# Second block's mixer: keys in three full blocks of 128, attention keys made with features as rows, index gemms first, and a buffer of its own for w_uk

## The chip, the cores and the metric

The kernel runs on one core of one Trainium2 chip. The metric is the device time of one execution in microseconds (us), as the median of several runs. The core's engines run side by side, each through its own queue in order: TensorE (PE, with its weight loads shown as PEld), VectorE (DVE), ScalarE (ACT), GpSimd (POOL), and SyncE (SP), which only issues DMAs. An instruction that waits holds up everything behind it in its own queue.

## What is computed

Two transformer blocks in float32 on 256 tokens of width 1024. The first block has four layers, the second has one, and 16 meta tokens are put ahead of its sequence, so it works on 272 positions. The change touches the second block's mixer, which stands between its two feed-forward stages. Cut to what matters:

```
u = rmsnorm(h, mix_norm) @ w_in                    # [272, 2632]
qa, ka, va, qb, ckv, iq, ik, iw = split(u)         # 512,512,512,512,256,512,64,8 wide

# attention A: 4 heads, two score maps each (m = 0, 1), 64 features per map
qa = rmsnorm(qa.reshape(272, 4, 2, 64), a_q_norm)
ka = rmsnorm(ka.reshape(272, 4, 2, 64), a_k_norm)  # 272 x 8 reciprocal roots
s  = einsum('qhmd,khmd->hmqk', qa, ka) * 64**-0.5 + bias_a   (causal)
p  = softmax(s);  a = p[:, 0] - lam * p[:, 1]
o_a = rmsnorm(a @ va, a_subln) * (1 - lam_init)

# attention B: an index picks 64 keys for each query, then 4 heads on a latent
q_lat = rmsnorm(qb @ w_uk, b_q_norm);  c = rmsnorm(ckv, b_kv_norm)
score = sum_h iw_h * relu(iq_h . ik * 64**-0.5)    (8 heads, causal)
sel   = top_k(score, 64)
p = softmax(q_lat . c[sel] * 256**-0.5 + bias_b);  o_b = (p @ c[sel]) @ w_uv

h = h + concat(o_a, o_b) @ w_out
```

Rows of queries are needed for the 256 tokens only; keys and values for all 272 positions.

## The kernel before, in words

Every large product is done in three passes (`mm3`, lines 225 to 227): the float32 operands are split into a rounded part and a remainder of type fp32r, and hi·hi, hi·lo and lo·hi are added up in PSUM (`acc`, four banks). Weights arrive through SP's queue as `raw` (three buffers of 128x2048); ACT rounds each into `hi` (line 73) and DVE forms `lo` (line 76), four buffers of each, in the order of a fixed plan. Between them stand small float32 matmuls and transposes with PSUM tiles `tp` (four banks).

In the second block the activations are held with the features as rows (`hT2`, `xT`). `FeatNorm.add` (lines 1114 to 1127) makes the next stage's operands for one block of 128 features and adds up the squares for the norm, on POOL (lines 1124 and 1126). `FeatNorm.rstd` turns the sums into the reciprocal root with a power of -0.5 on POOL (line 1142), as a column for each token and, after transposes, as a row `rrow`.

The mixer (`mixer2`) has a list of gemms in the order of `MIXER`: ka, qa, va, ik, iq, ckv, qb. Two forms exist. `gemm_as` puts tokens in rows: a block of 128 tokens is the stationary operand and 512 columns of weights stream past; ka and qa are made so. For ka that is three blocks of tokens (16, 128 and 128 of them, the first also computed as a full block), each with 24 matmuls of 512 columns. `gemm_ws` puts features in rows: 128 columns of weights are stationary, 272 or 256 tokens stream past; all others are made so. After a token-row gemm, `qk_sink` (lines 1571 to 1593) scales by the token's root, squares on ACT, sums by head on DVE (line 1583), takes the power of -0.5 of a 128x8 tile on POOL (line 1588 waits for it; the power itself is line 243 in a helper), multiplies on DVE (line 1588), and flips the block to features as rows with four PE transposes (line 1512).

Next to the gemms run small tasks held by `Tasks`, two steps after every gemm step: the index scores (`select_task`: dots on PE at line 1546, relu on ACT, weighted sum on DVE at 1549, then eight rounds of top-8 and replace for each of two query tiles at lines 1556 and 1557), units of attention A (`unit_a`: scores at line 1699, softmax with DVE line 1651 and ACT line 1652, flips at 1662, product with the values at 1673) and units of attention B (`unit_b`, scores at line 1731). Keys are handled in three parts of 16, 128 and 128 (`key_tiles`). The matrix w_uv is loaded at line 1430 into the buffer `wuk`; w_uk is loaded into the same buffer at line 1806, when the last use of w_uv is over. `finish` flips an output half for the last product with w_out (`mixer_out`).

The order of instructions on each engine is set by a scheduler when the program is built; what the queue order is can be listed from the program, and stands below where it matters.

Of the kernel before, what the change touches and what calls it, by code (L numbers as in the profile page):

```python
# [31 lines left out]

MIXER = ("ka", "qa", "va", "ik", "iq", "ckv", "qb")

# [119 lines left out]
def build(ctx, tc, A, out):  # L154
# [950 lines left out]
    class FeatNorm:  # L1105
# [9 lines left out]
        def add(self, f):  # L1115
            n, src = self.n, self.hT[:, f, self.c0:]
            g = self.g[:, f:f + 1]
            hi, lo = [xT[x][:, f, self.c0:] for x in ("hi", "lo")]
            nc.scalar.activation(hi, src, AF.Copy, scale=g)
            nc.vector.scalar_tensor_tensor(lo, src, g, hi.bitcast(F32), op0=ALU.mult, op1=ALU.subtract)  # L1120
            sq = self.pool.tile([P, KC], F32, tag="sqf", bufs=3, name=nm("sqf"))
            nc.scalar.activation(sq[:, :n], src, AF.Square)
            if f == 1:
                nc.gpsimd.tensor_add(self.sum[:, :n], self.prev[0][:, :n], sq[:, :n])
            elif 1 < f < KT - 1:
                nc.gpsimd.tensor_add(self.sum[:, :n], self.sum[:, :n], sq[:, :n])
            self.prev.append(sq)
# [57 lines left out]
    def bias_rows():  # L1185
# [3 lines left out]
        ra = npool.tile([8, NB_POS + 1], F32, name="ra")  # L1189
        frs = hpool2.tile([8, NB_POS], F32, name="frs")  # L1190
        nc.gpsimd.dma_start(rb, A["rel_bias_2"])
# [178 lines left out]
class Tasks:  # L1370
# [45 lines left out]
def mixer2(tc, nc, A, pool, E):  # L1416
# [21 lines left out]
    def lambda_task():  # L1438
        nc.vector.tensor_scalar(gs, gs, 1.0 - 0.2, None, op0=ALU.mult)
        es = []  # L1440
        for i in range(2):
            lj = pool.tile([P, 512], F32, tag="sq8", bufs=1, name=nm("lj"))[:, :64]
# [124 lines left out]
    def rq():  # L1567
        return pool.tile([P, 512], F32, tag="rq", bufs=5, name=nm("rq"))

    def qk_sink(name, g, dstT, cols):  # L1570
# [22 lines left out]
        return sink  # L1593

    va, vc = {}, {}

    def va_task():
        yield from need("vaT")
        for i, (T, (a, rows)) in enumerate(zip((2, 0, 1), tiles(KC))):
            tp = tp_bank()  # L1600
            for b in range(4):
                nc.tensor.transpose(tp[:rows, P * b:P * b + P], late["vaT"][:, b, a:a + rows], ident)
            va[T] = pool.tile([P, 512], F32, name=f"va{T}")
            nc.scalar.activation(va[T][:rows], tp[:rows], AF.Copy)
            yield True
        tk.flags.add("va")

    def vc_task(T):
        yield from need("cT")
        rows, c0 = ROWS[T], COL[T]  # L1610
        p_ = tp_bank()
        for k in range(2):
            nc.tensor.matmul(p_[:rows], lhsT=cT[:, k, c0:c0 + rows], rhs=wuv[:, k, :], start=k == 0, stop=k == 1)
        vc[T] = pool.tile([P, 512], F32, name=f"vc{T}")
        nc.scalar.activation(vc[T][:rows], p_[:rows], AF.Copy)
        tk.flags.add(("vc", T))
        yield True
# [205 lines left out]
    def gemms():  # L1823
# [47 lines left out]
def _layout(i):  # L1871
# [47 lines left out]
    for n, m in (("va", va), ("qb", qb), ("iq", iq), ("ckv", ckv)):  # L1919
        a["w2_" + n] = stat(m, 256)  # L1920
# [58 lines left out]
```

## Time and profile before

| | us |
|---|---|
| median of 3 runs | 2134.31 (2133.76 to 2134.83) |
| the profiled execution, its own time | 2134.71 |
| its span, first to last instruction | 2132.8 |
| granted TensorE clock over the span, share of full speed | 0.993 |
| the mixer: from the first matmul of ka to the last flip of the norm behind it | 1772.0 to 1943.0 of the span |

PE is busy in 99% of the span, DVE in 71%, ACT in 57% and POOL in 4%. A busy PE is not PE at its peak: matmuls overlap in their pipeline, so what one costs is the distance from its start to the next one's start and not its duration. POOL has 130 instructions in the whole program. Idle time of an engine that nobody waits for costs nothing. In the lists of instructions each row has the start in us from the span's start, the duration (of several rows merged: from the first start to the last end), the engine, the line, the operation, what is written and read with its shape, and in brackets the idle time ahead of it with what ended it.

### The profile page before, as it was taken

The numbers are of one execution on the slowest core, as the hardware profiler recorded it, in microseconds if no ns is written. First come the engines' busy times: TensorE is split into PE (matmuls) and PEld (weight loads), VectorE is DVE, ScalarE is ACT, GpSimd is POOL, SyncE is SP. The second block draws the span as 40 slices with busy tenths as digits, with TensorE's granted clock in tenths as the row PEclk, the third lists the DMA queues.
The fourth block names the chain that finished last, engine by engine and source line by source line (L and its number), as shares of the span: only waits on it lengthen the run. The fifth ranks groups of instructions, "written<-read, shape, count | busy, mean of one in ns | idle before, by whom it ended". The sixth has DMA issues, their size and how long they took to land.

```text
span 2132.8 us, 39626 instructions
## 1 busy us (share of the span) xinstructions
PE 2104.3 (99%) x15582; PEld 1974.8 (93%) x15582; DVE 1507.8 (71%) x3646; ACT 1216.2 (57%) x2355; POOL 95.5 (4%) x130
## 2 busy tenths in 40 slices
PE   8999999999999999999999999999999999999999
PEld 8999989989899889799889999899889998879999
DVE  6665679847799579699666655699666655667663
ACT  6656676635565466476455655666464445665442
POOL 1000000000000001100000000000010012011000
PEclk9999999999999999999999999999999999999999
DMA  7444545545465543155544444355556454414543
GB/s 258 149 151 150 177 148 196 181 159 189 165 217 198 197 163 101 39 192 205 190 160 167 149 151 162 124 214 179 197 159 246 142 177 171 140 50 139 189 152 115
DMA packets 57434, 352.37 MB, mean 165 GB/s; under 512 B 7232, under 2 KB 7776, under 8 KB 29728
## 3 DMA queue, kind: packets, MB, share of 16 engines
q1 hardware_dynamic: 53136, 338.88, 45.8%
q0 software_dynamic: 3824, 10.78, 1.7%
q8 instruction: 123, 2.02, 0.4%
q14 instruction: 63, 0.52, 0.1%
q10 hardware_dynamic: 288, 0.18, 0.0%
HBM read 348.74 MB, written 3.22 MB: 165 GB/s over the span
## 4 chain that ended last, share of the span: by engine, by line
PE 56%; DVE 5%; ACT 1%; POOL 1%; issue 1%; ACTq 0%; POOLq 0%; DVEq 0%
PE acc L225 17%; PE acc L227 17%; PE acc L226 17%; DVE lo L76 1%; DVE cvh L1024 1%; DVE o L1024 1%; POOL s L243 1%; PE tp L1673 1%; PE tp L840 1%; PE tp L782 0%; PE tp L1001 0%; PE tp L827 0%; PE tp L802 0%; PE tp L306 0%; ACT hi L73 0%
## 5 line engine op out<-in xcount | busy, mean ns | idle before, releaser
L76 DVE TENSOR_TENSOR lo<-raw,hi 128x512 fp32r<-128x512 f32 (+2 forms) x1440 | 855.3, 633 | 326.6 <-ACT hi L73 322.7
L73 ACT ACTIVATE hi<-raw 128x1024 fp32r<-128x1024 f32 (+3 forms) x720 | 672.5, 965 | 431.3 <-issue 193.3
L227 PE MATMUL acc<-xhi,lo 128*128 128x256 f32 (+1 forms) x2432 | 690.4, 284 | 0.0
L226 PE MATMUL acc<-xlo,hi 128*128 128x256 f32 (+1 forms) x2432 | 690.1, 284 | 0.0
L225 PE MATMUL acc<-xhi,hi 128*128 128x256 f32 (+1 forms) x2432 | 689.8, 284 | 0.2 <-DVE u L515 0.2
L227 PEld LDWEIGHTS acc<-xhi,lo 128*128 128x128 f32 x2432 | 461.9, 190 | 1.1 <-issue 0.9
L225 PEld LDWEIGHTS acc<-xhi,hi 128*128 128x128 f32 x2432 | 461.4, 190 | 1.0 <-issue 0.4
L226 PEld LDWEIGHTS acc<-xlo,hi 128*128 128x128 f32 x2432 | 459.0, 189 | 1.0 <-issue 0.6
L225 PE MATMUL acc<-hi,xhi 128*128 128x384 f32 (+2 forms) x920 | 317.7, 346 | 1.5 <-ACT xhi L348 1.4
L227 PE MATMUL acc<-hi,xlo 128*128 128x384 f32 (+2 forms) x920 | 307.9, 335 | 0.0
L226 PE MATMUL acc<-lo,xhi 128*128 128x384 f32 (+2 forms) x920 | 306.6, 333 | 0.0
L225 PE MATMUL acc<-hi,hidh 128*128 128x512 f32 x480 | 190.7, 398 | 0.3 <-ACT hidh L230 0.3
L227 PE MATMUL acc<-hi,hidl 128*128 128x512 f32 x480 | 189.6, 395 | 0.0
L226 PE MATMUL acc<-lo,hidh 128*128 128x512 f32 x480 | 189.4, 395 | 0.0
L225 PEld LDWEIGHTS acc<-hi,xhi 128*128 128x128 f32 x920 | 172.8, 188 | 9.8 <-ACT xhi L348 3.2
L227 PEld LDWEIGHTS acc<-hi,xlo 128*128 128x128 f32 x920 | 172.7, 188 | 2.5
L226 PEld LDWEIGHTS acc<-lo,xhi 128*128 128x128 f32 x920 | 173.2, 188 | 1.9
L243 POOL TENSOR_TENSOR s<-s,neghalf 128x1 f32<-128x1 f32 (+5 forms) x56 | 42.4, 759 | 1546.6 <-DVE s L256 1415.2
L225 PEld LDWEIGHTS acc<-hi,hidh 128*128 128x128 f32 x480 | 90.5, 189 | 20.6 <-ACT hidh L230 0.5
L227 PEld LDWEIGHTS acc<-hi,hidl 128*128 128x128 f32 x480 | 90.4, 188 | 19.7
L226 PEld LDWEIGHTS acc<-lo,hidh 128*128 128x128 f32 x480 | 90.5, 188 | 19.3
L225 PE MATMUL acc<-hidh,hi 128*128 128x272 f32 (+1 forms) x352 | 100.6, 286 | 0.0
(342 smaller groups left out, 2534.7 us busy)
## 6 DMA issues: line engine op xcount, KB each, us to landing
raw<-in_ffn_w_in_dram SPq DMA_DIRECT2D x88, 1024.0 KB, 4.9
raw<-in_attn_w_qkv_dram SPq DMA_DIRECT2D x96, 768.0 KB, 4.2
raw<-in_ffn_w_out_dram SPq DMA_DIRECT2D x44, 1024.0 KB, 4.9
raw<-in_ffn_w_gu_dram SPq DMA_DIRECT2D x44, 1024.0 KB, 4.9
raw<-in_ffn_w_dn_dram SPq DMA_DIRECT2D x32, 704.0 KB, 4.1
raw<-in_sc_w_in_dram SPq DMA_DIRECT2D x16, 768.0 KB, 4.2
raw<-in_cc_w_pw_dram SPq DMA_DIRECT2D x12, 1024.0 KB, 4.9
raw<-in_attn_w_o_dram SPq DMA_DIRECT2D x8, 1024.0 KB, 4.9
```

Of the source, the lines that this page charges most:

```text
L73: nc.scalar.activation(hi[:, sl], raw[:, sl], AF.Copy)
L76: nc.vector.tensor_sub(lo[:, s2], raw[:, s2], hi[:, s2].bitcast(F32))
L225: nc.tensor.matmul(o, lhsT=lh[0], rhs=rh[0], start=first, stop=False)
L226: nc.tensor.matmul(o, lhsT=lh[0], rhs=rh[1], start=False, stop=False)
L227: nc.tensor.matmul(o, lhsT=lh[1], rhs=rh[0], start=False, stop=last)
L243: mark["pow"] = nc.gpsimd.tensor_tensor(r[:parts], m[:parts], neghalf[:parts, :w], op=ALU.pow)
L840: nc.tensor.matmul(o[rows, 64 * hh:64 * hh + 64], lhsT=pT[s, T][hh][:, j, rows], rhs=vals if h2 is None else vals[:, c, hh, :], start=i == ...
L1024: nc.vector.scalar_tensor_tensor(d, x, w, other, op0=ALU.mult, op1=ALU.add)
L1673: nc.tensor.matmul(o[:, :P], lhsT=pT[:rows, i, :], rhs=vals[t][:rows, P * hd:P * hd + P], start=i == 0, stop=i == len(kts) - 1)
```

## The change

1. `MIXER` becomes ik, iq, ka, qa, va, ckv, qb: the two gemms of the index come first.
2. ka is made with `gemm_ws`: four groups of 128 features by 272 tokens, each with 24 matmuls. Its norm is done in that form: ACT squares the group (128x272), one float32 matmul with a 0/1 matrix `pair` adds up each head's 64 rows and spreads the sum over them, DVE scales and adds the epsilon (line 1620 of the changed kernel), POOL takes the power of -0.5 of the whole 128x272 tile (line 1621), and DVE multiplies (line 1625). The three flips of ka on PE go. qa stays as it was.
3. Keys are handled in blocks of 128 that begin at 0, 128 and 144 (`KB`). The third overlaps the second in 112 keys, so its first 112 value rows are zeroed on POOL (`value_block`); for the first query tile two blocks do, and the probabilities of keys 144 to 255 are zeroed on POOL.
4. w_uk gets a buffer of its own and is loaded at the start of the mixer, behind w_uv, on POOL's queue.
5. The sums of squares in `FeatNorm.add` move from POOL to DVE (both uses, ahead of the mixer and behind it).
6. To make room, scratch tiles share one buffer with the table `frs` of the bias, and the pool `rq` has four buffers where it had five.

```diff
-MIXER = ("ka", "qa", "va", "ik", "iq", "ckv", "qb")
+MIXER = ("ik", "iq", "ka", "qa", "va", "ckv", "qb")
...
             if f == 1:
-                nc.gpsimd.tensor_add(self.sum[:, :n], self.prev[0][:, :n], sq[:, :n])
+                nc.vector.tensor_add(self.sum[:, :n], self.prev[0][:, :n], sq[:, :n])
             elif 1 < f < KT - 1:
-                nc.gpsimd.tensor_add(self.sum[:, :n], self.sum[:, :n], sq[:, :n])
+                nc.vector.tensor_add(self.sum[:, :n], self.sum[:, :n], sq[:, :n])
...
+    wuk = pool.tile([P, 4, 256], F32, tag="wuk", bufs=1, name="wuk")
+    nc.gpsimd.dma_start(wuk, A["b_w_uk_2"])
...
+    KB = [0, P, KC - P]
+
+    def value_block(name, i, src):
+        t = pool.tile([P, 512], F32, name=f"{name}{i}")
+        nc.scalar.activation(t, src, AF.Copy)
+        if i == 2:
+            for rows in (slice(0, 96), slice(96, 3 * P - KC)):
+                nc.gpsimd.memset(t[rows], 0.0)
+        return t
...
+    def ka_sink(u, ps):
+        nc.vector.tensor_mul(kaT[:, u, :], ps[:, :KC], rrow)
+        tk.add(ka_task(u))
+
+    def ka_task(u):
+
+        k = kaT[:, u, :]
+        sq, R = [pool.tile([P, KC], F32, tag="rl", bufs=3, name=nm("kn")) for _ in range(2)]
+        nc.scalar.activation(sq, k, AF.Square)
+        yield True
+        st = tp_bank()
+        nc.tensor.matmul(st[:, :KC], lhsT=pair, rhs=sq, start=True, stop=True)
+        nc.vector.tensor_scalar(R, st[:, :KC], 1.0 / 64, EPS, op0=ALU.mult, op1=ALU.add)
+        nc.gpsimd.tensor_tensor(R, R, E["neghalf"][:, 0:1].to_broadcast([P, KC]), op=ALU.pow)
+        yield True
+        for _ in range(LAG):
+            yield False
+        nc.vector.scalar_tensor_tensor(k, k, gk, R, op0=ALU.mult, op1=ALU.mult)
+        done_k.append(u)
+        if len(done_k) == 4:
+            tk.flags |= {("ka", t) for t in range(3)}
+        yield True
...
+    def gemm_ka():
+        for u in range(2):
+            yield from gemm_ws("w2_ka", u, 2, 0, lambda t, ps: ka_sink(2 * u + t, ps))
...
         ns = pool.tile([P, KC], F32, tag="ns2", bufs=6, name=nm("ns2"))
+        if n < KC:
+            nc.gpsimd.memset(ns[:, n:2 * P], 0.0)
...
     def gemm_qb():
-        tk.until(("dots", 0), ("dots", 1), ("vc", 0), ("vc", 1), ("vc", 2))
-        wuk = pool.tile([P, 4, 256], F32, tag="wuk", bufs=1, name="wuk")
-        nc.gpsimd.dma_start(wuk, A["b_w_uk_2"])
+        tk.until(("dots", 0), ("dots", 1))
...
-            "ka": lambda: gemm_as("w2_ka", (0, 1, 2), 512, 4, qk_sink("ka", gk, kaT, COL)),
+            "ka": gemm_ka,
```

POOL's queue before, from the powers of the norm ahead of the mixer (`rcol`) on; `s` with 8 columns are the tokens' roots of ka (three) and qa (two):

```order
L1430 DMA wuv<-in_b_w_uv_dram 128x1024
L1142 TENSOR_TENSOR rcol_20516<-s_20524,neghalf 16x1
L1142 TENSOR_TENSOR rcol_20516<-s_20530,neghalf 128x1
L1142 TENSOR_TENSOR rcol_20516<-s_20536,neghalf 128x1
L243 TENSOR_TENSOR s_20642<-s_20640,neghalf 128x8
L243 TENSOR_TENSOR s_20664<-s_20662,neghalf 128x8
L243 TENSOR_TENSOR s_20686<-s_20684,neghalf 16x8
L243 TENSOR_TENSOR s_20768<-s_20766,neghalf 128x8
L243 TENSOR_TENSOR s_20797<-s_20795,neghalf 128x8
L243 TENSOR_TENSOR s_21345<-s_21344,neghalf 16x1
```

The same queue now, behind the load of w_uk and four more memsets of `ns`; `kn` is the tile R of a feature group of ka:

```order
L1695 MEMSET ns_3219_21349 128x112
L1695 MEMSET ns_3223_21357 128x112
L1621 TENSOR_TENSOR kn_20774<-kn_20774,neghalf 128x272
L1621 TENSOR_TENSOR kn_20807<-kn_20807,neghalf 128x272
L1621 TENSOR_TENSOR kn_20850<-kn_20850,neghalf 128x272
L1621 TENSOR_TENSOR kn_20884<-kn_20884,neghalf 128x272
L243 TENSOR_TENSOR s_20980<-s_20978,neghalf 128x8
L243 TENSOR_TENSOR s_21002<-s_21000,neghalf 128x8
L1530 MEMSET va_21265 96x512
L1530 MEMSET va_21265 16x512
L243 TENSOR_TENSOR s_21310<-s_21309,neghalf 16x1
```

Five powers of 8 columns have become two, with four powers of 272 columns ahead of them. DVE's queue now, from the first group of ka to the first index scores; `acc` is the gemm's bank, `lo` the remainder of a weight that a later gemm needs (20889 is va's first weight):

```order
L1609 TENSOR_TENSOR kaT<-acc_20747,rrow_20541 128x272
L1620 TENSOR_SCALAR kn_20774<-tp_20776 128x272
L1625 SCALAR_TENSOR_TENSOR kaT<-kaT,headgains,kn_20774 128x272
L1609 TENSOR_TENSOR kaT<-acc_20780,rrow_20541 128x272
L76 TENSOR_TENSOR lo_20889<-raw_20737,hi_20888 128x512 x2
L1620 TENSOR_SCALAR kn_20807<-tp_20809 128x272
L76 TENSOR_TENSOR lo_20889<-raw_20737,hi_20888 128x512 x2
L1609 TENSOR_TENSOR kaT<-acc_20823,rrow_20541 128x272
L1625 SCALAR_TENSOR_TENSOR kaT<-kaT,headgains,kn_20807 128x272
L1620 TENSOR_SCALAR kn_20850<-tp_20852 128x272
L1625 SCALAR_TENSOR_TENSOR kaT<-kaT,headgains,kn_20850 128x272
L1609 TENSOR_TENSOR kaT<-acc_20856,rrow_20541 128x272
```

Each multiplication at line 1625 waits for POOL's power of its group, and the next group's first step stands behind it: group 2 behind power 1, group 4 behind power 3. Right behind these rows stand the four `lo` of va's second weight, the fourth `kn` (line 1620) and the fourth multiplication (line 1625), and only then the index scores. Before, the same stretch of DVE's queue was, from the first block of ka:

```order
L1583 TENSOR_REDUCE s_20638<-sq_3094_20636 128x8
L247 TENSOR_SCALAR s_20640<-s_20638 128x8
L1588 TENSOR_TENSOR rq_20634<-rq_20634,s_20642 128x512
L1583 TENSOR_REDUCE s_20660<-sq_3099_20658 128x8
L247 TENSOR_SCALAR s_20662<-s_20660 128x8
L1588 TENSOR_TENSOR rq_20656<-rq_20656,s_20664 128x512
```

Here too the multiplication (line 1588) waits for a power, of 8 columns. The buffers of `kn` come from the pool `rl` of three, which the index scores use as well: the third relu of the index takes the buffer of the fourth group's `kn`.

PE's queue now, at the fourth group: `pair` is the 0/1 matrix, the gemm on either side is qa's, and behind it come the first four of the 32 index dots:

```order
L227 MATMUL acc_20896<-hi_20739,xlo_19771 128x512
L1619 MATMUL tp_20910<-kn_20883,pair 128x272
L225 MATMUL acc_20897<-hi_20739,xhi_19770 128x512
L226 MATMUL acc_20897<-lo_20740,xhi_19770 128x512
L227 MATMUL acc_20897<-hi_20739,xlo_19771 128x512
```

The matmul with `pair` needs the square of the fourth group, and all that follows on PE stands behind it; before, this place had qa's matmuls with the flips of ka (line 1512) between them. Behind the four dots PE's queue has 24 more matmuls of qa, 24 of va's first group, four dots, and then va's second group.

## Rows read from the trace of the kernel before

**Rows 1.** The page's head, and busy us, share and instructions of each engine.

```profile
span 2132.8 us, 39626 instructions
...
PE 2104.3 (99%) x15582; PEld 1974.8 (93%) x15582; DVE 1507.8 (71%) x3646; ACT 1216.2 (57%) x2355; POOL 95.5 (4%) x130
```

**Rows 2.** Stretches: length, busy us of each engine, granted clock, DMA share, GB/s.

```profile
1880.00:1890.00 10.00, 7.51 (x32) 4.37 (x31) 9.16 (x45) 5.39 (x10) 1.40 (x2) 0.83 0.16 53
...
1920.00:1943.00 23.00, 21.97 (x171) 20.93 (x170) 17.70 (x37) 13.81 (x28) 7.09 (x8) 0.96 0.27 93
```

**Rows 3.** Waits of PE in 1771 to 1943: total, times, longest.

```profile
PE tp L1627 <- DMA wuk<-in_b_w_uk_dram: 2.5, 1, 2.5
PE tp L1137 <- POOL sqsum L1126: 1.0, 1, 1.0
...
PE tp L1143 <- POOL rcol L1142: 0.7, 1, 0.7
```

**Rows 4.** POOL's groups by shape, whole span: busy us, mean ns of one, idle before.

```profile
L243 POOL TENSOR_TENSOR s<-s,neghalf 128x1 f32<-128x1 f32 x44 | 27.0, 615 | 1448.5 <-DVE s L256 1415.2 <-DVE s L247 20.2 <-DVE rope_nh L635 13.2
...
L243 POOL TENSOR_TENSOR s<-s,neghalf 128x8 f32<-128x8 f32 x4 | 7.0, 1746 | 17.6 <-DVE s L247 17.6
L1126 POOL TENSOR_TENSOR sqsum<-sqsum,sqf 128x272 f32<-128x272 f32 x5 | 5.5, 1108 | 36.8 <-ACT sqf L1122 36.8
...
L243 POOL TENSOR_TENSOR s<-s,neghalf 128x4 f32<-128x4 f32 x4 | 4.0, 1011 | 26.6 <-DVE s L247 26.6
```

**Rows 5.** POOL in order of time: a power of 8 columns and one of 1.

```profile
1788.03 1.66 POOL L243 TENSOR_TENSOR s<-s,neghalf 128x8 f32<-128x8 f32 x1 [9.88 <-DVE s L247]
...
1898.27 0.55 POOL L243 TENSOR_TENSOR s<-s,neghalf 128x1 f32<-128x1 f32 x1 [4.06 <-DVE s L247]
```

**Rows 6.** PE in order of time, in the mixer.

```profile
1772.00 0.48 PE L225 MATMUL acc<-hi,xhi 128*128 128x512 f32 x1
...
1784.02 0.39 PE L225 MATMUL acc<-hi,xhi 128*128 128x512 f32 x1
...
1793.53 0.40 PE L227 MATMUL acc<-hi,xlo 128*128 128x512 f32 x1
1793.77 0.60 PE L1512 MATMUL tp<-ident,rq 128*128 128x128 f32 x4
1794.12 0.48 PE L225 MATMUL acc<-hi,xhi 128*128 128x512 f32 x1
...
1803.65 0.29 PE L226 MATMUL acc<-xlo,hi 128*128 128x272 f32 x1
...
1806.55 0.29 PE L225 MATMUL acc<-xhi,hi 128*128 128x272 f32 x1
...
1825.16 0.28 PE L226 MATMUL acc<-xlo,hi 128*128 128x256 f32 x1
...
1827.74 0.28 PE L227 MATMUL acc<-xhi,lo 128*128 128x256 f32 x1
...
1851.33 1.42 PE L1546 MATMUL tp<-ikT,iqT 64*128 64x272 f32 x7
...
1868.51 0.41 PE L227 MATMUL acc<-xhi,lo 128*128 128x256 f32 x1
...
1871.92 0.41 PE L225 MATMUL acc<-xhi,hi 128*128 128x256 f32 x1
...
1916.06 2.00 PE L1731 MATMUL tp<-cT,qlT 128*128 128x272 f32 x8
```

**Rows 7.** DVE in order of time: lo of one weight, the multiplication behind a power, one 128x272 product.

```profile
1783.97 2.50 DVE L76 TENSOR_TENSOR lo<-raw,hi 128x512 fp32r<-128x512 f32 x4 [4.24 <-ACT hi L73]
...
1789.72 0.69 DVE L1588 TENSOR_TENSOR rq<-rq,s 128x512 f32<-128x512 f32 x1 [1.77 <-POOL s L243]
...
1807.08 0.43 DVE L1791 TENSOR_TENSOR vaT<-acc,rrow 128x272 f32<-128x272 f32 x1
```

**Rows 8.** ACT in order of time: the square of one 128x272 tile.

```profile
1840.45 0.42 ACT L1492 ACTIVATE sqk<-cT 128x272 f32<-128x272 f32 x1
```

More of the change, by code (lines that the diff above doesn't have):

```diff
@@ L1189, in bias_rows @@
         ra = npool.tile([8, NB_POS + 1], F32, name="ra")
-        frs = hpool2.tile([8, NB_POS], F32, name="frs")
+        frs = hpool2.tile([P, NB_POS], F32, tag="frs", bufs=1, name="frs")[:8]
         nc.gpsimd.dma_start(rb, A["rel_bias_2"])
@@ L1441, in lambda_task @@
         for i in range(2):
[L1442 removed]
+            lj = E["hpool2"].tile([P, NB_POS], F32, tag="frs", bufs=1, name=nm("lj"))[:, :64]
             s_, e_ = small(), small()
@@ L1567, in rq @@
     def rq():
-        return pool.tile([P, 512], F32, tag="rq", bufs=5, name=nm("rq"))
+        return pool.tile([P, 512], F32, tag="rq", bufs=4, name=nm("rq"))
     def qk_sink(name, g, dstT, cols):
@@ L1593, in qk_sink @@
         return sink
+    def ka_sink(u, ps):
[18 more added lines that the diff above has]
+        yield True
+    done_k = []
+    pair = pool.tile([P, P], F32, name="pair")
+    nc.vector.memset(pair, 0.0)
+    for i in range(2):
+        nc.vector.memset(pair[64 * i:64 * i + 64, 64 * i:64 * i + 64], 1.0)
+    def gemm_ka():
+        for u in range(2):
+            yield from gemm_ws("w2_ka", u, 2, 0, lambda t, ps: ka_sink(2 * u + t, ps))
     va, vc = {}, {}
@@ L1598, in va_task, with vc_task @@
         yield from need("vaT")
-        for i, (T, (a, rows)) in enumerate(zip((2, 0, 1), tiles(KC))):
+        for i, a in enumerate(KB):
             tp = tp_bank()
             for b in range(4):
-                nc.tensor.transpose(tp[:rows, P * b:P * b + P], late["vaT"][:, b, a:a + rows], ident)
-            va[T] = pool.tile([P, 512], F32, name=f"va{T}")
-            nc.scalar.activation(va[T][:rows], tp[:rows], AF.Copy)
+                nc.tensor.transpose(tp[:, P * b:P * b + P], late["vaT"][:, b, a:a + P], ident)
+            va[i] = value_block("va", i, tp)
             yield True
         tk.flags.add("va")
-    def vc_task(T):
+    def vc_task(i):
         yield from need("cT")
-        rows, c0 = ROWS[T], COL[T]
+        c0 = KB[i]
         p_ = tp_bank()
         for k in range(2):
[L1613 to L1616, printed above, removed]
+            nc.tensor.matmul(p_, lhsT=cT[:, k, c0:c0 + P], rhs=wuv[:, k, :], start=k == 0, stop=k == 1)
+        vc[i] = value_block("vc", i, p_)
+        tk.flags.add(("vc", i))
         yield True
@@ L1653, in softmax @@
         return ns, den
-    def key_tiles(T):
-        return [(2, 0, META), (0, META, P)] + ([(1, META + P, P)] if T else [])
     def flip_p(p_sb, T):
-        kts = key_tiles(T)
+        m = 2 + T
         pt = tp_bank()
-        for i, (t, k0, rows) in enumerate(kts):
-            nc.tensor.transpose(pt[:rows, P * i:P * i + P], p_sb[:, k0:k0 + rows], ident)
+        for i in range(m):
+            nc.tensor.transpose(pt[:, P * i:P * i + P], p_sb[:, KB[i]:KB[i] + P], ident)
         pT = pool.tile([P, 3, P], F32, tag="pT2", bufs=2, name=nm("pT2"))
-        nc.scalar.activation(pT[:META, 0, :], pt[:META, :P], AF.Copy)
-        m = len(kts) - 1
-        nc.scalar.activation(pT[:, 1:1 + m, :].rearrange("p a b -> p (a b)"), pt[:, P:P + m * P], AF.Copy)
+        nc.scalar.activation(pT[:, :m].rearrange("p a b -> p (a b)"), pt[:, :m * P], AF.Copy)
         return pT
     def weigh(pT, T, vals, hd):
-        kts = key_tiles(T)
+        m = 2 + T
         o = tp_bank()
-        for i, (t, k0, rows) in enumerate(kts):
-            nc.tensor.matmul(o[:, :P], lhsT=pT[:rows, i, :], rhs=vals[t][:rows, P * hd:P * hd + P], start=i == 0, stop=i == len(kts) - 1)
+        for i in range(m):
+            nc.tensor.matmul(o[:, :P], lhsT=pT[:, i, :], rhs=vals[i][:, P * hd:P * hd + P], start=i == 0, stop=i == m - 1)
         return o[:, :P]
@@ L1744, in finish @@
         if half not in oT:
-            oT[half] = [pool.tile([P, 4, S], F32R, tag=t, bufs=1, name=nm("oT")) for t in (("qaT", "kaT"), ("iqb", "wuk"))[half]]
+            oT[half] = [pool.tile([P, 4, S], F32R, tag=t, bufs=1, name=nm("oT")) for t in (("qaT", "kaT"), ("iqb", "wuv"))[half]]
         tp = tp_bank()
@@ L1782, in done_b @@
     def done_b(T):
-        yield from need(("B", T), *[("ql", hd, t) for hd in range(4) for t in range(2)])
+        yield from need(("B", T), *[("ql", hd, t) for hd in range(4) for t in range(2)], *[("vc", i) for i in range(3)])
         finish(outs["B", T], 1, T)
@@ L1912, in _layout @@
     qa, ka, va, qb, ckv, iq, ik, iw = [w[:, o[j]:o[j + 1]] for j in range(8)]
-    for n, m in (("qa", qa), ("ka", ka)):
-        a["w2_" + n] = mov(m, 4)
+    a["w2_qa"] = mov(qa, 4)
     def stat(m, cols):
         return m.reshape(8, P, m.shape[1] // cols, cols).transpose(2, 1, 0, 3).reshape(-1, P, 8 * cols)
-    for n, m in (("va", va), ("qb", qb), ("iq", iq), ("ckv", ckv)):
+    for n, m in (("ka", ka), ("va", va), ("qb", qb), ("iq", iq), ("ckv", ckv)):
         a["w2_" + n] = stat(m, 256)
```

4 lines of the change are left out of this document (2 added, 2 removed).

## The prediction, made before the changed kernel ran

> **What bounds the kernel now.** The page's head comes first [rows 1]: PE is busy in 99% of 2132.8 us, POOL in 4%. The change lies in the mixer, 1772 to 1943 us, so the stretches there come next. PE is nearly full there too, also in the stretch where it is emptiest, 1880 to 1890 us, where it is busy for 7.51 of 10 us at a clock of 0.83 [rows 2]. PE's waits in the mixer [rows 3] are few: 2.5 us for the load of w_uk, 1.0 us for POOL's sum of squares, 0.7 us for the norm's roots. So the mixer is bound by the number and width of PE's matmuls, at these distances from start to start [rows 6]: 512 columns (1793.53 - 1784.02)/41 = 0.232 us; 272 columns (1806.55 - 1803.65)/23 = 0.126; 256 columns (1827.74 - 1825.16)/22 = 0.117; and while the clock is low, 256 columns take (1871.92 - 1868.51)/16 = 0.213. Whoever takes columns from PE gains, as long as no other queue becomes later than PE. That is why POOL's list is read last, although it is the idlest engine: the change gives it a new kind of work.
>
> **What PE saves.** ka had 3 x 24 matmuls of 512 columns, 72 x 0.232 = 16.7 us; now 4 x 24 of 272 columns, 96 x 0.126 = 12.1 us: 4.6 us less. Three flips go, 1794.12 - 1793.77 = 0.35 us each [rows 6], 1.1 us. Four matmuls with `pair` come, float32 and 272 columns, 2.00/8 = 0.25 us each in the nearest row [rows 6] and some 0.2 us more for going from the gemm to them and back, an estimate from the longer start-to-start distances around small matmuls: 1.8 us. Together -3.9 us. The wait for w_uk goes (-2.5 us): loaded at the start of the mixer, it is there 100 us ahead of its first use. The sums of squares on DVE take away the wait of 1.0 us; the six adds are about 0.43 us each on DVE (as the 128x272 product in [rows 7]), 2.6 us in a stretch where DVE works 17.7 of 23 us [rows 2], so they fit, and ahead of the mixer DVE has more room still (71% over the span [rows 1]). With the index's gemms first, the selection's 16 rounds on DVE no longer crowd the stretch where DVE is busy for 9.16 of 10 us; what that gives PE is at most the clock and the idle time there that is not w_uk's, 0 to 5 us, and I take 2, near the 0.17 x 10 us that the clock lost in that stretch. Costs nothing: the third key block and the zeroing (as many matmuls as before, each of the same columns, ACT loses 16 small copies), four `rq` buffers for five (ka no longer uses them), the shared scratch buffer. If POOL did nothing else, the sum would be -3.9 - 2.5 - 1.0 - 2 = -9.4 us: 2134.7 - 9.4 = 2125.3.
>
> **What POOL is given.** Before, ka and qa gave POOL five powers of 8 columns, one for each token block. Now ka gives it four powers of 272 columns, a value for every token and every row, though each root stands there 64 times over. The trace has no such instruction; it has the same operation at 1, 4 and 8 columns. Undisturbed, 1 column takes 0.55 us and 8 columns 1.66 us [rows 5], so a column costs (1.66 - 0.55)/7 = 0.159 us, and 272 columns 0.55 + 271 x 0.159 = **43.5 us**. The groups' means bracket it [rows 4]: 0.615 us for 1 and 1.011 for 4 columns give 0.132 a column and 36.4 us; 1.746 for 8 against 0.55 for 1 gives 0.171 and 46.9 us. Far below lies an add of 128x272 on the same engine, 1.108 us [rows 4]: so moving the data is not what costs in the power, the power is. I take 43.5: it is the same operation on the same engine, and 1, 4 and 8 columns lie near one line.
>
> A rule of the Trainium skill speaks for the cheap end: "GPSIMD Engine Reference", section "Elementwise — side-by-side cycle accounting", gives a two-input elementwise instruction about 2.6 cycles per element at 1.2 GHz, which by that page would be an estimate of 0.6 us for 272 columns. The add of 1.108 us here is of that size, the powers of 8 columns with 1.66 us are not; by that rule the sum would stay at 2125, by the rows it does not.
>
> **Where these powers stand, and who waits.** All four stand in a row in POOL's queue. DVE's queue has the multiplication by each power in it, and behind it the next group's steps; PE's queue has the matmul with `pair` of groups 2 and 4 behind those. So nothing runs past them. Step by step: PE begins at 1772.0. The norm's small matmuls cost 2.3 us among the first 42 matmuls (1784.02 - 1772.00 - 42 x 0.232 [rows 6]); then ik 24 x 0.126 = 3.0, iq 96 x 0.117 = 11.2, ka's first group 3.0: 1791.5. Product 0.43 [rows 7], square 0.42 [rows 8], `pair` half way through the second group, scale and epsilon 0.43: the first power starts at about 1794.5. Between power 1 and 2: multiplication 0.5, the second group's product 0.43, square 0.42, `pair` 0.5, scale 0.43, and some 0.15 us for each of four hand-overs: 2.9 us. Between 2 and 3, whose `pair` is already done: 1.2. Between 3 and 4: multiplication, product, the four `lo` of a weight, 2.50 us [rows 7], scale: 4.1. After 4 one multiplication, 0.5. End of the chain: 1794.5 + 4 x 43.5 + 8.7 = **1977.2 us**.
>
> PE in the meantime gets as far as its second set of dots: the third dot needs a bank whose relu waits for the fourth `kn`'s buffer. With 0.9 us for relu and dots, va's second group starts at 1978.1. In the trace of before it starts at 1806.55 [rows 6]: 171.5 us later. By then the changed kernel has done what the old one had still ahead: ik and iq, 14.2 us, and six of 32 dots at 1.42/7 = 0.2 us [rows 6], 1.2 us. What follows in both is the same work (rest of va, ckv, qb, the units of A and B, w_out). Less the waits named above, 3.5, and the 2 us of the selection; more for PE's clock, which fell to half after short idle times in the mixer: after idle times of 40 us I count a restart of 28 matmuls at 0.213 for 0.117, 2.7 us.
>
> Sum: +171.5 - 15.4 - 3.5 - 2.0 + 2.7 = **+153.3 us**. The 4.6 us of ka's gemm are in the first term. Against the profiled execution's own 2134.71 us, which is 0.4 us over the median of the runs: 2288.0, or 2287.6 by the median; I say **2288**.
>
> **The rivals.** (1) The power costs what an add costs, 1.1 us, because what the 8-column rows show is a start-up cost that grows over the first columns only. Then the chain runs beside PE, nothing waits, and the time is 2125.3: faster. For it speaks the add's row; against it that 1, 4 and 8 columns show no flattening. The point from which it decides: PE would come to va's second group at 1772.0 + 2.3 + 14.2 + 12.1 + 1.8 + 11.1 (qa, 48 x 0.232) + 0.8 + 3.0 = 1817.3, and the chain lets it through at 1794.5 + 4p + 8.7 + 0.9; the wait 4p - 13.2 eats the 9.4 us at p = 5.7 us. So a power of 272 columns under a seventh of my price means faster. Chance 0.08. (2) The price per column falls with length, say to half: 4 x 21.7 us less, 2201. No row shows it. Chance 0.06. (3) A power near 5.7 us, so no difference to be seen: 0.02. (4) Dearer than the bracket, since DVE's work beside POOL lengthens a power (1.746 in the mean against 1.66 undisturbed): but DVE stands still for most of each power here. Over 2310: 0.02.
>
> **How the numbers follow.** My forecast has 0.82. Its own ends: price 36.4 us, 4 x 7.1 = 28 us less; 46.9 us, 14 us more; the selection's 0 to 5 us and the restart make some 3 us below and 6 above: 2257 to 2308. I give 2257 to 2310; what it leaves out are the four rivals, 0.18. A difference of 0.2% (4.3 us) is about what a measurement of this kernel can tell from none. Faster by more than that is rival 1, 0.08; within it rival 3, 0.02; slower my forecast, rival 2 and rival 4, 0.90.
>
> **What would show it.** In the changed kernel's profile POOL's busy time rises from 95.5 us to about 255, with one group of four powers 128x272 at 43.5 us each; PE has three long waits, put down to ACT's squares or DVE's multiplications behind the powers, some 160 us together (4p - 13.2 with p = 43.5); the first power starts near 1794.5, va's second group near 1978. PE's matmuls of ka take 0.126 us from start to start; no wait for w_uk is left. Powers of about 1 us, and a time under 2130, would show that I was wrong on the one number that all hangs on; powers of 43 us without PE waiting would show that I misread the queues.

## The result, and the profile after

The changed kernel takes 2292.76 us (median of 4 runs, 2290.64 to 2293.69), against 2134.31 for the kernel before: a ratio of 1.0741, 95% interval 1.0722 to 1.0760. It is slower by 158.4 us. The prediction said 2288, between 2257 and 2310.

The page of the changed kernel, in the lines that answer to [rows 1] and [rows 4]: the head, the engines' busy time, three of the rows of 40 slices, the chain of work that ended last, and three groups (busy us, mean ns of one, idle time of the engine before them).

```profile
span 2291.8 us, 39670 instructions
...
PE 2105.3 (92%) x15602; PEld 1979.9 (86%) x15602; DVE 1506.8 (66%) x3664; ACT 1209.9 (53%) x2334; POOL 255.2 (11%) x135
...
PE   9999999999999999999999999999999312489999
...
POOL 1000000000000011000000000001000799620000
PEclk9999999999999999999999999999999755799999
...
PE 51%; POOL 8%; DVE 5%; ACT 1%; issue 1%; ACTq 0%; DVEq 0%; POOLq 0%
...
L1621 POOL TENSOR_TENSOR kn<-kn,neghalf 128x272 f32<-128x272 f32 x4 | 175.2, 43806 | 24.6 <-DVE kn L1620 24.6
...
L1619 PE MATMUL tp<-kn,pair 128*128 128x272 f32 x8 | 3.9, 580 | 123.6 <-ACT kn L1616 123.6
L1625 DVE SCALAR_TENSOR_TENSOR kaT<-kaT,headgains,kn 128x272 f32<-128x272 f32 x4 | 2.0, 502 | 172.7 <-POOL kn L1621 172.7
```

The span is 159.0 us longer, and PE is busy for 1.0 us more only: nothing was added to its work, it stands still. Where its row of slices falls to 3, 1, 2 and 4, POOL's row rises to 7, 9, 9 and 6. Four instructions account for POOL's rise from 95.5 us [rows 1] to 255.2. The chain that ended last, in which POOL now has 8%, runs through them.

POOL in order of time (start, us, operation; in brackets the idle time before it):

```profile
1796.27 43.75 POOL L1621 TENSOR_TENSOR kn<-kn,neghalf 128x272 f32<-128x272 f32 x1 [16.29 <-DVE kn L1620]
1843.26 44.08 POOL L1621 TENSOR_TENSOR kn<-kn,neghalf 128x272 f32<-128x272 f32 x1 [3.24 <-DVE kn L1620]
1888.31 43.70 POOL L1621 TENSOR_TENSOR kn<-kn,neghalf 128x272 f32<-128x272 f32 x1 [0.97 <-DVE kn L1620]
1936.12 43.70 POOL L1621 TENSOR_TENSOR kn<-kn,neghalf 128x272 f32<-128x272 f32 x1 [4.12 <-DVE kn L1620]
```

PE's waits in 1765 to 2110 us (total, times, longest), and PE in order of time at the end of each long wait, with the first matmul of the mixer ahead:

```profile
PE tp L1619 <- ACT kn L1616: 123.6, 3, 80.7
PE tp L1559 <- ACT rl L1561: 31.2, 3, 30.7
PE tp L1705 <- DVE ns L1748: 6.1, 3, 5.0
PE tp L1514 <- ACT ql L1678: 2.1, 2, 1.9
```

```profile
1773.74 0.33 PE L225 MATMUL acc<-xhi,hi 128*72 128x272 f32 x1
...
1841.42 1.28 PE L1619 MATMUL tp<-kn,pair 128*128 128x272 f32 x2 [42.70 <-ACT kn L1616]
...
1933.47 1.27 PE L1619 MATMUL tp<-kn,pair 128*128 128x272 f32 x2 [80.74 <-ACT kn L1616]
...
1980.79 0.84 PE L1559 MATMUL tp<-ikT,iqT 64*128 64x144 f32 x2 [30.68 <-ACT rl L1561]
...
1982.69 0.59 PE L225 MATMUL acc<-xhi,hi 128*128 128x272 f32 x1
```

PE waits 42.70, 80.74 and 30.68 us. The rows name ACT's squares and relus; what is late is the POOL power ahead of the DVE multiplication ahead of them: DVE sat idle for 172.7 us before its four multiplications of line 1625, until POOL's `kn` was there. The waits of [rows 3] for w_uk and for the sum of squares are gone. In their place stands one that the kernel before did not have: 6.1 us for DVE's `ns`, the weighted scores of a softmax unit.

### The profile page after: what moved, and what is told of

It reads as the page before. It is cut to its first block, busy times and chain, and to the rows that moved or that the text cites. A ratio compares the mean times of both kernels' runs of the same rounds, so it can differ in the third digit from the quotient of the medians.

```text
span 2291.8 us, 39670 instructions
## 1 busy us (share of the span) xinstructions
PE 2105.3 (92%) x15602; PEld 1979.9 (86%) x15602; DVE 1506.8 (66%) x3664; ACT 1209.9 (53%) x2334; POOL 255.2 (11%) x135
## 4 chain that ended last, share of the span: by engine, by line
PE 51%; POOL 8%; DVE 5%; ACT 1%; issue 1%; ACTq 0%; DVEq 0%; POOLq 0%
PE acc L225 15%; PE acc L226 15%; PE acc L227 15%; POOL kn L1621 8%; DVE lo L76 1%; DVE cvh L1024 1%; DVE o L1024 1%; PE tp L840 1%; POOL s L243 1%; PE tp L782 0%; PE tp L1001 0%; PE tp L827 0%; PE tp L1714 0%; PE tp L802 0%; ACT hi L73 0%
## 5 line engine op out<-in xcount | busy, mean ns | idle before, releaser
L227 PE MATMUL acc<-xhi,lo 128*128 128x256 f32 (+1 forms) x2464 | 700.4, 284 | 0.0
L225 PE MATMUL acc<-xhi,hi 128*128 128x256 f32 (+1 forms) x2464 | 699.2, 284 | 0.3 <-DVE u L515 0.3
L226 PE MATMUL acc<-xlo,hi 128*128 128x256 f32 (+1 forms) x2464 | 699.4, 284 | 0.0
L225 PEld LDWEIGHTS acc<-xhi,hi 128*128 128x128 f32 x2464 | 467.6, 190 | 2.6 <-issue 1.9
L227 PEld LDWEIGHTS acc<-xhi,lo 128*128 128x128 f32 x2464 | 468.3, 190 | 0.3
L225 PE MATMUL acc<-hi,xhi 128*128 128x384 f32 (+2 forms) x896 | 310.1, 346 | 1.5 <-ACT xhi L348 1.4
L227 PE MATMUL acc<-hi,xlo 128*128 128x384 f32 (+2 forms) x896 | 299.6, 334 | 0.0
L226 PE MATMUL acc<-lo,xhi 128*128 128x384 f32 (+2 forms) x896 | 298.3, 333 | 0.0
L243 POOL TENSOR_TENSOR s<-s,neghalf 128x1 f32<-128x1 f32 (+4 forms) x53 | 35.6, 673 | 1484.5 <-DVE s L256 1416.4
L1621 POOL TENSOR_TENSOR kn<-kn,neghalf 128x272 f32<-128x272 f32 x4 | 175.2, 43806 | 24.6 <-DVE kn L1620 24.6
L1625 DVE SCALAR_TENSOR_TENSOR kaT<-kaT,headgains,kn 128x272 f32<-128x272 f32 x4 | 2.0, 502 | 172.7 <-POOL kn L1621 172.7
```

The costliest lines, as they stand in the source:

```text
L225: nc.tensor.matmul(o, lhsT=lh[0], rhs=rh[0], start=first, stop=False)
L226: nc.tensor.matmul(o, lhsT=lh[0], rhs=rh[1], start=False, stop=False)
L227: nc.tensor.matmul(o, lhsT=lh[1], rhs=rh[0], start=False, stop=last)
L243: mark["pow"] = nc.gpsimd.tensor_tensor(r[:parts], m[:parts], neghalf[:parts, :w], op=ALU.pow)
L1621: nc.gpsimd.tensor_tensor(R, R, E["neghalf"][:, 0:1].to_broadcast([P, KC]), op=ALU.pow)
L1625: nc.vector.scalar_tensor_tensor(k, k, gk, R, op0=ALU.mult, op1=ALU.mult)
```

## The experiments

Ratios are of runs to those of the kernel before on the same chip, with 95% intervals. Differences in us are of medians.

**e1: the price alone.** A multiplication of the same shape in place of the power (the roots are left out):

```diff
-        nc.gpsimd.tensor_tensor(R, R, E["neghalf"][:, 0:1].to_broadcast([P, KC]), op=ALU.pow)
+        nc.gpsimd.tensor_tensor(R, R, E["neghalf"][:, 0:1].to_broadcast([P, KC]), op=ALU.mult)
```

> The four 128x272 powers of ka on POOL become multiplications by -0.5 of the same shape, with the same broadcast operand, at the same place in the queue; the reciprocal roots of ka's norm are left out by that, nothing else. My theory (the power itself costs the time, 43.8 us each): POOL's four instructions take about 1.1 us each like the adds of that shape before, no wait of PE behind them is left, and the time falls to 2125 us (2121 to 2130), so 9 us under the kernel before. Rival theory (the broadcast operand, the tile's width or the place in POOL's queue costs the time): the instructions stay tens of us long and the time stays over 2200.

Measured: 2130.14 us, ratio 0.9971 (0.9959 to 0.9982), 6.7 us less than before's 2136.83. POOL's group, PE's waits in the mixer, and two stretches (length, busy us of PE, PEld, DVE, ACT, POOL, granted clock, DMA share, GB/s):

```profile
L1621 POOL TENSOR_TENSOR kn<-kn,neghalf 128x272 f32<-128x272 f32 x4 | 2.9, 733 | 26.8 <-DVE kn L1620 26.8
```

```profile
PE tp L1705 <- DVE ns L1748: 6.0, 3, 5.0
PE tp L1514 <- ACT ql L1678: 2.1, 2, 1.9
PE acc L225 <- ACT oT L230: 1.1, 1, 1.1
```

```profile
1860.00:1870.00 10.00, 6.20 (x40) 4.43 (x39) 9.44 (x54) 8.11 (x28) 2.25 (x4) 0.99 0.10 43
1870.00:1880.00 10.00, 7.63 (x26) 5.36 (x27) 7.36 (x32) 4.67 (x17) 2.35 (x4) 0.67 0.21 68
```

One word takes away all of the loss: the four powers, and nothing else in the change, make it slow. The rest of the change gains, but 6.7 us, not the 9.4 of the prediction. The wait for `ns` is here as well, so the powers don't make it; the longest part of it begins in the stretch where DVE is busy for 9.44 of 10 us, about half of that with the selection's rounds, and in the next stretch PE's clock is at 0.67.

**e2: the curve of the price.** The four powers with 34, 68, 136 and 272 columns (the other columns keep no root):

```diff
+        w = (34, 68, 136, KC)[u]
+        nc.gpsimd.tensor_tensor(R[:, :w], R[:, :w], E["neghalf"][:, 0:1].to_broadcast([P, w]), op=ALU.pow)
```

> The four powers of ka cover 34, 68, 136 and 272 columns of their tiles; the other roots are left out. My theory (a fixed price for each column, and a chain of the four that nothing runs past): 0.55 us and 0.159 us for each further column, so 5.8, 11.2, 22.0 and 43.7 us, together 92 us less than four of 272 columns, and the time falls by the same 92 us from 2292.8 to 2201 (2195 to 2208). Rival (the price per column falls with length): the 136 columns take clearly less than 22 us and the prices bend; rival (POOL's chain is only part of the path): the time falls by clearly less than the powers do.

Measured: 2199.12 us (one run). POOL in order of time:

```profile
1793.96 5.85 POOL L1622 TENSOR_TENSOR kn<-kn,neghalf 128x34 f32<-128x34 f32 x1 [16.30 <-DVE kn L1620]
1803.05 11.61 POOL L1622 TENSOR_TENSOR kn<-kn,neghalf 128x68 f32<-128x68 f32 x1 [3.24 <-DVE kn L1620]
1815.62 22.04 POOL L1622 TENSOR_TENSOR kn<-kn,neghalf 128x136 f32<-128x136 f32 x1 [0.96 <-DVE kn L1620]
1841.77 43.70 POOL L1622 TENSOR_TENSOR kn<-kn,neghalf 128x272 f32<-128x272 f32 x1 [4.12 <-DVE kn L1620]
```

A column costs (11.61 - 5.85)/34 = 0.169, then (22.04 - 11.61)/68 = 0.153 and (43.70 - 22.04)/136 = 0.159 us. It doesn't get cheaper with length, which was rival 2. The powers took 83.2 us in all, 92.0 us less than in the changed kernel, and the time fell by 93.6 us: what the powers take, PE waits.

**e3: the point from which it decides.** All four powers with 33 columns, by the prediction the width at which gain and wait cancel (the other columns keep no root):

```diff
+        w = 33
+        nc.gpsimd.tensor_tensor(R[:, :w], R[:, :w], E["neghalf"][:, 0:1].to_broadcast([P, w]), op=ALU.pow)
```

> All four powers of ka cover 33 columns of their tiles, the other roots are left out: the width at which the prediction puts the break-even, 0.55 + 32 x 0.159 = 5.6 us each. My theory: PE still waits about 9 us in all behind the powers, which eats what the other parts of the change gain, and the time is that of the kernel before, 2134 (2130 to 2138). Rival (a power of this length is hidden beside PE's other work, because PE and DVE have more slack than I counted): 2126, as with no power at all.

Measured: 2144.14 us, ratio 1.0035 (1.0021 to 1.0048): 7.3 us slower, not level. POOL's group and PE's wait behind it, and three stretches:

```profile
L1622 POOL TENSOR_TENSOR kn<-kn,neghalf 128x33 f32<-128x33 f32 x4 | 23.1, 5768 | 24.6 <-DVE kn L1620 24.6
```

```profile
PE tp L1619 <- ACT kn L1616: 10.0, 3, 5.2
```

```profile
1795.00:1805.00 10.00, 5.36 (x31) 4.90 (x30) 3.56 (x8) 2.44 (x3) 6.49 (x2) 0.76 0.21 90
1805.00:1815.00 10.00, 8.13 (x46) 7.17 (x44) 1.66 (x4) 1.49 (x2) 9.03 (x2) 0.89 0.32 105
1815.00:1825.00 10.00, 6.66 (x18) 4.97 (x20) 3.69 (x7) 1.81 (x3) 5.88 (x2) 0.66 0.29 105
```

The wait is what 4p - 13.2 gives for p = 5.77 us: 9.9, measured 10.0. Yet e3 is 14.0 us slower than e1, 4.0 more than the wait. What the prediction's balance left out is the clock: two waits of some 5 us leave it at 0.76, 0.89 and 0.66 in three stretches where e1 has 1.00. That the clock makes all of the 4.0 us is argued, not shown. And the other side of the balance is 6.7 us, not 9.4. By a straight line from p = 3.3 (no wait, -6.7) to 5.77 (+7.3), the point lies near 4.5 us, an estimate.

**e4: the same roots, made once.** One root for each token and head, 6 columns for each feature group; DVE spreads each over 64 columns, PE transposes it, and the multiplication reads the result from PSUM:

```diff
-        nc.tensor.matmul(st[:, :KC], lhsT=pair, rhs=sq, start=True, stop=True)
...
+        for i, a in enumerate(KB):
+            nc.tensor.matmul(st[:, 2 * i:2 * i + 2], lhsT=sq[:, a:a + P], rhs=pair, start=True, stop=True)
+        m, r = small(6), small(6)
+        nc.vector.tensor_scalar(m, st[:, :6], 1.0 / 64, EPS, op0=ALU.mult, op1=ALU.add)
+        power(r, m, 6)
...
+        nc.vector.tensor_copy(rx.rearrange("p (a b) -> p a b", a=6), r[:, :, None].to_broadcast([P, 6, 64]))
+        R = tp_bank()
+        for i, a in enumerate(KB):
+            nc.tensor.transpose(R[:, a:a + P], rx[:, P * i:P * i + P], ident)
```

> ka's features stay as rows, but the roots are taken once for each token and head: twelve matmuls give the sums of squares with tokens as rows, POOL takes four powers of 128x6, DVE spreads each root over 64 columns, and twelve transposes bring them back. Nothing of the computation is left out. My theory: each power takes 0.55 + 5 x 0.159 = 1.35 us and hides beside PE's work; PE pays some 2 us for the small matmuls; the time is 2127 us (2123 to 2131), under the kernel before. Rival (the longer chain through PE, DVE, POOL, DVE, PE holds PE up in its queue, as the flips of the old form did not): 2134 or more.

Measured: 2132.40 us, ratio 0.9979 (0.9970 to 0.9988), 4.4 us less than before. That is 1.4 us outside the range of my theory and short of the rival's 2134. POOL's group:

```profile
L243 POOL TENSOR_TENSOR s<-s,neghalf 128x6 f32<-128x6 f32 x4 | 5.7, 1424 | 24.1 <-DVE s L1622 24.1
```

The new layout of ka can be had without the loss. The gain is again some 3 us under the prediction's sum, so the next four runs took its small terms one by one.

**f1: e4 with the old order of the gemms** (ka, qa, va, ik, iq, ckv, qb):

> e4_token_roots with its gemms in the order of the kernel before (ka, qa, va first, then ik, iq), all else as in e4. Theory A, the prediction's term: index gemms first take the selection's rounds out of a crowded stretch, worth 2 us; so this kernel is 2 us slower than e4's difference of -4.4 us, about -2.4 us. Theory B: with the index gemms first the units of A lose the gemms beside them, and a new wait of PE for the softmax's scaled scores (6.0 us, longest 5.0) takes back more than that; then the old order has no such wait and is faster than e4: about -8 us. The wait of PE in the units' pair matmuls for the softmax shows which.

Measured: 2129.86 us, ratio 0.9966 (0.9952 to 0.9979), 6.0 us less than before's 2135.89. Theory A fails. The wait for `ns` is gone, as theory B has it, but the gain is short of its 8 us, and as the intervals of f1 and e4 overlap, it isn't shown that f1 is the faster of the two.

**f2: the kernel before with w_uk in its own buffer:**

> The kernel before with one part alone: w_uk in a buffer of its own, loaded at the start of the mixer (its room comes from the shared scratch buffer and four rq buffers for five). Theory A, the prediction's term: PE's wait of 2.5 us goes and nothing takes its place, -2.5 us. Theory B: in that stretch the selection on DVE is late anyway, so that PE's next wait grows by what this one gave; then 0 to -1 us.

Measured: 2137.75 us, ratio 1.0009 (1.0001 to 1.0018), 1.9 us more: no gain, which is against theory A, and not even the small one of theory B.

**f3: the kernel before with the index gemms first:**

> The kernel before with one part alone: the index gemms first. Theory A, the prediction's term: -2 us. Theory B: PE gets a new wait for the softmax in the units of A, about 5 us, and gains the clock and the crowded stretch only in part: +1 to +4 us.

Measured: 2149.89 us, ratio 1.0060 (1.0048 to 1.0073), 14 us slower: the direction of theory B, far beyond its 4 us.

**f4: the kernel before with the sums of squares on DVE:**

> The kernel before with one part alone: the six adds of squares on DVE in place of POOL. Theory A, the prediction's term: the wait of 1.0 us for POOL's sum in the mixer goes, -1.0 us, and the same place in the other stages gives nothing. Theory B: the squares of ACT and the root after the sum are the later end of that wait, so the wait stays under another name: 0 us.

Measured: 2133.20 us, ratio 0.9986 (0.9977 to 0.9995), 2.7 us less: theory A's direction, with more than its size.

PE's waits in 1765 to 1960 us, first of f2, then of f1, then of f3:

```profile
PE tp L1629 <- DVE oT L1757: 3.0, 1, 3.0
```

```profile
PE tp L1678 <- DVE oT L1803: 3.8, 1, 3.8
```

```profile
PE tp L1662 <- DVE s L1706: 4.9, 1, 4.9
PE tp L1627 <- DMA wuk<-in_b_w_uk_dram: 4.4, 1, 4.4
```

In f2 the same matmuls with w_uk wait 3.0 us for a bank that DVE empties into `oT`, behind the selection's rounds: the wait for the load (2.5 us) had covered it. DVE in order of time, one of the last rounds and the first write into `oT`:

```profile
1890.53 0.30 DVE L1558 MAX8 m<-score 128x8 f32<-128x144 f32 x1
...
1891.23 0.74 DVE L1757 SCALAR_TENSOR_TENSOR oT<-tp,headgains,oT 128x512 fp32r<-128x512 f32 x1
```

In f4 the wait for the sum is gone, but behind the wait for w_uk (2.6 us) stands one of 1.2 us for that bank, which the kernel before doesn't have. So PE's waits don't explain the gain of 2.7 us; its interval, 1.1 to 4.9 us, lies just above the 1.0 of the prediction. In f3 the order alone brings a new wait of 4.9 us, makes the one for w_uk longer, and costs 14 us.

**g1, g2: two orders in between**, e4 with ka, ik, iq, qa, va, ckv, qb and with ka, qa, ik, iq, va, ckv, qb:

> e4_token_roots with the order ka, ik, iq, qa, va, ckv, qb. Theory A, the queue that ends last moves with the order: with index first PE waits 6.0 us for the softmax of the units of A, with index last 3.8 us for a bank that DVE frees behind the selection's rounds. Between the two, ka's roots have the index gemms beside them and the selection starts some 14 us later than with index first and 11 us earlier than with index last: each of the two waits is there in part, and the difference to the kernel before is between -8 and -6 us. Theory B, only the start of the selection counts: the wait for the softmax stays as long as index stands ahead of va, -4 us.

> e4_token_roots with the order ka, qa, ik, iq, va, ckv, qb. Theory A: ka and qa are normalised beside the index gemms, the units of A begin right behind va with ckv and qb still ahead of PE; the waits are again in between, -8 to -6 us. Theory B, as for the order with ka alone in front: -4 us.

Measured: g1 2135.33 us, ratio 0.9997 (0.9988 to 1.0006); g2 2137.97, ratio 1.0010 (1.0001 to 1.0019). Both theories fail: the middle is worse than either end. **g3: f1 without the buffer of its own for w_uk:**

> f1_token_old_order without the buffer of its own for w_uk: the load stands where the kernel before has it. Theory A, the waits lie over each other: behind the wait of 2.5 us for w_uk stands the wait of 3.8 us for the bank that DVE frees behind the selection's rounds, so taking the buffer away costs nothing, within 1 us of f1's difference of -6.0 us. Theory B, the prediction's term: w_uk's wait is worth 2.5 us of its own, so -3.5 us.

Measured: 2129.38 us, ratio 0.9967 (0.9955 to 0.9979), 6.2 us less than before's 2135.59. It has f2's pair of waits the other way round, 2.9 us for the load and 0.4 for the bank:

```profile
PE tp L1676 <- DMA wuk<-in_b_w_uk_dram: 2.9, 1, 2.9
...
PE tp L1676 <- DVE oT L1801: 0.4, 1, 0.4
```

So the buffer is worth nothing here: as one wait goes, the other takes its time. All four of these kernels (before and f2, g3 and f1) have the index last. With the index first, as in the changed kernel, no run takes the buffer away alone; f3, which has that order, waits 4.4 us for w_uk.

What the orders do is seen in PE's gemm matmuls (`acc`), the work that stands ready to fill waits. Here is the last one before the longest gap in them and the first one behind it (`oT` is the output projection), in order of time on PE; first of f1, then of e4, then of g1, then of f3:

```profile
1874.46 0.28 PE L227 MATMUL acc<-xhi,lo 128*128 128x256 f32 x1
...
1882.05 0.73 PE L225 MATMUL acc<-oT,hi 128*128 128x256 f32 x4 [0.33 <-ACT oT L1802]
```

```profile
1865.58 0.28 PE L227 MATMUL acc<-xhi,lo 128*128 128x256 f32 x1
...
1894.58 0.75 PE L225 MATMUL acc<-oT,hi 128*128 128x256 f32 x3
```

```profile
1859.24 0.28 PE L227 MATMUL acc<-xhi,lo 128*128 128x256 f32 x1
...
1896.97 1.01 PE L225 MATMUL acc<-oT,hi 128*128 128x256 f32 x3 [0.35 <-ACT oT L1802]
```

```profile
1868.88 0.28 PE L227 MATMUL acc<-xhi,lo 128*128 128x256 f32 x1
...
1905.47 0.39 PE L225 MATMUL acc<-oT,hi 128*128 128x256 f32 x1
```

The gap is 7.6 us in f1, 29.0 in e4, 37.7 in g1 and 36.6 in f3. With the index last, the units of A are done early, and their output projection fills in between the units of B. With the index ahead of them, the input gemms run out before A is done, and for some 30 us PE has only small matmuls; in e4 its clock there is at 0.72, 0.94 and 0.83 in three stretches of 10 us from 1870 on. Among these kernels with token roots, a longer gap goes with a longer time: -6.0 us at 7.6, -4.4 at 29.0, -0.3 at 37.7, and +2.4 for g2, at 37.5 (1861.79 to 1899.24). It isn't in proportion: from f1 to e4 the gap grows by 21.4 us and the time by 1.6, from e4 to g1 by 8.7 and some 4. That the gap is the cause isn't shown, since no run changed it alone; nor why g1 and g2 have a longer one than e4.

**g4: rows or columns.** The changed kernel with each power made on 16 rows (the other 112 keep no root):

```diff
+        nc.gpsimd.tensor_tensor(R[:16], R[:16], E["neghalf"][:16, 0:1].to_broadcast([16, KC]), op=ALU.pow)
```

> The changed kernel with each of the four powers made on 16 rows in place of 128, the other 112 rows left without their root. If the price goes by columns alone, a power stays at 43.8 us and the time at 2293 us. If it goes by elements, a power takes an eighth of that, 5.5 us, and the time is near 2134 us.

Measured: 2293.9 us (one run). POOL in order of time, the first power:

```profile
1796.56 43.74 POOL L1621 TENSOR_TENSOR kn<-kn,neghalf 16x272 f32<-16x272 f32 x1 [16.30 <-DVE kn L1620]
```

An eighth of the elements, the same 43.74 us: columns are the price. That each root stood there 64 times over in rows cost nothing; that tokens were columns cost everything.

## Why the prediction was right

**The price of a power**, 43.5 us worked out from 1 and 8 columns, measured 43.7 to 44.1: 1.2 us more over four. That 1, 4 and 8 columns lie on one line held for 34 times the length, and the steeper and flatter lines (46.9, 36.4) came from group means, in which longer instructions are mixed with the undisturbed ones (1 column takes 0.615 us in the mean, 0.55 undisturbed).

**The queues.** The first power was to start at 1794.5 and started at 1796.27. That isn't an error of the chain: the mixer's first gemm began at 1773.74, not 1772.00, and from there to the power it took 22.53 us, forecast 22.5. (The mixer's start varies by more than that between the kernels run here, as the last section shows. The wait of 1.0 us for the sum of squares has no part in it: in the trace of before it ends at 1939.34, behind the mixer.) The matmuls of ka start 0.126 us apart, as forecast. The gaps between powers, 3.24, 0.97 and 4.12 us, were forecast as 2.9, 1.2 and 4.1. The four took 175.2, and with the last multiplication (0.50) the chain ended at 1980.35, forecast 1977.2. The long waits come to 154.1 us, forecast some 160.

**From there on.** va's second group starts at 1982.69, 4.6 us later than forecast: 1.8 from the start, 1.4 from the chain, 1.4 from relu and dots, which took 2.3 us and not 0.9: the granted clock was at 0.50, and the second relu stood behind the rounding of a weight on ACT (1.05 us). Behind it the changed kernel needs 2291.8 - 1982.69 = 309.1 us, the one before 2132.8 - 1806.55 = 326.2 [rows 1, 6]: 17.1 less. The forecast has 18.2 less (15.4 + 3.5 + 2.0 - 2.7). So of the 5.7 us between the forecast's +153.3 and the span's +159.0, 4.6 lie up to va's second group and 1.1 behind it.

**The terms that were mis-sized** are the small ones. By e1 the rest of the change is worth 6.7 us and not 9.4, which is 2.7 of the 5.1 us between the forecast of +153.3 and the measured +158.4; the powers make the other 2.4. That the error of the small terms is no larger is luck, since one by one they were wrong, and 174 us of powers hide it. The 2.5 us for w_uk are 0 with the index last, where f2 and g3 show another wait underneath; with the index first that stays open. The selection's 2 us have the wrong sign in f3, where the order costs 14 us; between f1 and e4 it is 1.6 us, not clear of noise. The crowded stretch of [rows 2] didn't go, it moved; in the changed kernel it is this one, and PE is emptier in it than before:

```profile
2030.00:2040.00 10.00, 4.75 (x23) 3.39 (x22) 9.44 (x51) 5.45 (x23) 2.64 (x6) 0.75 0.00 0
```

The sum of squares gave 2.7 where 1.0 was forecast. What is left for ka's new form and the key blocks, f1 less f4, is about -3.3 us with the cost of token roots in it, if the parts add up and with some 3 us of noise; forecast -3.9 without that cost. The step that failed is in "What PE saves": it read the wait that came last and the busiest stretch, but not what was queued next behind them.

**Rival 1** (2125.3 if the power cost as little as an add) came true in e1 in kind: with a multiplication of 0.733 us nothing waits behind POOL, and the kernel is faster; in size by 6.7, not 9.4 us. Rival 2 fell with e2. Of rival 3, the point at which it decides, the wait was right to 0.1 us, but not the balance (e3).

The rule of the Trainium skill that the prediction weighed ("GPSIMD Engine Reference", section "Elementwise — side-by-side cycle accounting") would be an estimate of 0.6 us for 272 columns by its 2.6 cycles at 1.2 GHz. The multiplication with 0.733 us is of that size; the power of the same shape, with 43.8 us, is not.

## What to carry to other kernels

Price each operation of an idle engine by rows of that operation, not of a cheaper one with the same shape: on POOL a power of 272 columns took 60 times a multiplication, and a mean over the span (POOL busy in 4%) didn't warn of it. Before a layout is turned, count the columns of the expensive step: here 272 in place of 6 or 8 for the same roots. And before a wait is booked as a gain, look for the next one behind it, and for whether gemm work is left to stand beside what then becomes late.

## What the runs showed of the chip

- POOL's power costs columns, not rows: 43.74 us on 16 rows, 43.75 on 128. Over the widths 6, 33, 34, 68, 136 and 272 it took 1.42, 5.77, 5.85, 11.61, 22.04 and 43.70 us.
- On POOL a multiplication by a value spread over 272 columns took 0.733 us, the add of two full tiles 1.108 [rows 4].
- After two waits of about 5 us PE's granted clock fell to 0.66 in a stretch of 10 us (e3). After the wait of 30.68 us in the changed kernel, the granted clock was 0.50 from 1983 to 1987 us (the lower of its two levels, 1.2 GHz): matmuls of 272 columns started 0.226 us apart, 20 times, and then 0.126 again. That cost 2.0 us, forecast 2.7.
- The start of the mixer differs by up to 3.3 us between the kernels profiled here (first gemm at 1771.18 in f4, 1774.49 in g2), and by 2.6 us between two that differ only in the powers behind it (1771.42 in e2, 1774.03 in g4). Terms of 1 or 2 us can't be read from two profiled spans alone.
